# A streaming encoder step on one core: how the first conditioning rows are loaded, placed and stored

## The chip, the cores and the metric

The kernel runs on one core of a Trainium2 chip. The metric is the device time of one execution in microseconds (us). TensorE is called PE here, VectorE DVE, ScalarE ACT, GpSimd POOL and SyncE SP; SP does no arithmetic and issues most of the transfers.

## The reference

A prompt of 512 frames and eight running streams of 16 frames each (640 rows of width 2048 in all) pass through two layers, stick-breaking attention and gated linear attention. Each layer first normalises its input and shifts and scales it by a conditioning vector, one for the prompt and one for each stream. What matters for the change is that first step of the first layer:

```python
shift, scale, gate = jnp.split(c @ w_ada[i] + b_ada[i], 3, axis=-1)
h = rmsnorm(x, norm_g[i]) * (1 + scale[:, None]) + shift[:, None]
q, k, v, zg = jnp.split(h @ w_in, 4, axis=-1)
```

All is float32. `c @ w_ada` multiplies nine rows by a matrix of 2048 x 4096 for shift and scale (32 MiB in float32), so that it is a matter of moving the matrix, hardly of arithmetic.

## The kernel before

The 640 rows lie turned: rows of h (2048 of them, 16 tiles of 128) on the partitions, the 640 frames along the free dimension. To keep float32 accuracy, PE multiplies in the rounded type float32r, and each operand is split into a rounded part and a remainder (`halves`, line 133: ACT makes the rounded part, DVE the remainder), so that one product takes three matmuls.

**The beginning** (lines 758 to 848) does these things one after the other or woven together.

- x is loaded in ten pieces of 512 KB into tiles s0 to s9 of the pool `sp` (line 766). Between the first and the second pair of pieces stand six small loads: the norm weights and the bias (`crow`), and the conditioning vectors (`c9`). For each of the five groups of 128 frames (line 781), ACT squares and sums the pieces in four parts, PE turns 16 blocks, and DVE and ACT copy them out of PSUM. The reciprocal root is taken on GpSimd, and PE spreads it over the partitions (`turned_wide`, line 246).
- The conditioning matrix is taken in eight **blocks** (`ada0`, line 821, which calls `ada_mod`, line 161). A block gives shift and scale for two of the 16 tiles of h and has 4 MiB. It is loaded in 4 groups; each group is followed on PE by its small products (L180: the matrix's piece streams past the nine conditioning rows). Blocks 0, 1, 6 and 7 come alone, in pieces of 256 KB with runs of 1 KB; blocks 2 and 3, and 4 and 5, come as pairs, in pieces of 512 KB with runs of 2 KB. The pieces go round in a ring of eight tiles (s10 to s15 and two tiles `ar`), for block 6 of six, for block 7 of four (lines 817 to 819). When a block's products are done, DVE copies the sums out of PSUM (L185), PE turns them (L189), DVE adds the bias and makes scale and shift (L198 to L200).
- Then `scale` (line 405) makes two tiles of h of them (`mod`, two buffers), `part_up` (line 412) stores a half of one of them to device memory (L415, issued by ACT, ahead of the splits) and splits them, and `add_up` makes sums that later products want and writes them to tiles s2j and s2j+1 for block j.
- The **product** of block j (L519, in `six`, line 488) multiplies its two tiles of h by 512 columns of `w_in`: five groups of 128 frames, called fifths below, each with six matmuls of 512 columns. Its weights (`wr`, 512 KB) are asked for two products ahead, and their tile is free when the weights before them have been split (`wl`, L135).

After the last product begin the large ones, by a scheme with seven products in place of eight (L595, in `by_sevens`, line 529). They and all that follows are not touched by the change.

**What sets the order.** PE's queue runs in the order in which the program is written (line 81). To choose it, the program keeps a clock of its own, `pe["now"]`: each operation adds what it is held to cost (`by`, line 54), and a class `Side` (line 277) runs a side task's next step when that clock has reached its due time. For the conditioning the due time of a group comes from `pace` (line 806): the clock at which the n-th piece of 512 KB is held to have landed. The other engines and SP run in the order that the compiler's scheduler chooses, except from the end of block 7's products on, where DVE, ACT and GpSimd run as written (line 834). A queue runs strictly in order, so that a group whose piece hasn't landed holds up whatever stands behind it on PE, and a load whose tile isn't free holds up the loads behind it on SP.

Of the kernel before, what the change touches and what calls it, by code (L numbers as in the profile page):

```python
# [41 lines left out]
def hybrid_step_kernel(ctx: ExitStack, tc: tile.TileContext, A: dict, O: list):  # L42
# [4 lines left out]
    dve = nc.vector  # L47


    pe = {"now": 0.0, "quad": 4800}  # L50

    mm, turn_block = nc.tensor.matmul, nc.tensor.transpose

# [11 lines left out]
    def block(x):  # L65

        pe["now"] += 0.11
        return x
# [92 lines left out]
    def ada_mod(pool, ring, i, j0, ns, tag, group, pace=None, close=None):  # L161
# [21 lines left out]
            close()  # L183
        row = pool.tile([P, 256], F32, tag="ada_r", name="ada_r")[:, :w]
        dve.tensor_copy(row, acc[:, :w])  # L185
        yield step(1.5 if pace else 4.0, tp=1)
        tp = bank("tp")
        for s in range(ns):
            turn_block(tp[:, P * s:P * s + P], block(row[:, P * s:P * s + P]), ident)  # L189
# [38 lines left out]
    def rstd_of(pool, ss, n, name):  # L228
# [4 lines left out]
        r = pool.tile([P, w], F32, tag=name + "_r", name=name + "_r")  # L233
        nc.gpsimd.tensor_tensor(r, ms, mhalf[:, :w], op=ALU.pow)
        return r

    def rstd_row(pool, ss, bc, a):

        turned_wide(wide_of(pool, rstd_of(pool, ss, D, "nrm")), bc, a)

    def wide_of(pool, r):
        wide = pool.tile([P, P], F32, tag="rstd_w", name="rstd_w", bufs=2)
# [31 lines left out]
    def step(wait=0.0, tp=0, z=0, tiled=False):  # L274
        return wait, tp, z, tiled
# [111 lines left out]
    class Quarters:  # L387
# [24 lines left out]
        def part_up(self, i, j, two):  # L412

            (a0, a1), b = [self.exact[j][0][:, c] for c in hs], self.exact[j][1]
            nc.scalar.dma_start(out=h21_d[i][:, j, :], in_=a1)  # L415
            self.lower[j], self.upper[j] = slot(j, (P, 2, HALF)), slot(8 + j, (P, 2, HALF))
            self.whole[j] = slot(16 + 2 * j), slot(17 + 2 * j)
            halves(self.lower[j][:, 0], self.lower[j][:, 1], a0)
            halves(self.upper[j][:, 0], self.upper[j][:, 1], a1)
            halves(*self.whole[j], b)  # L420
            self.middle[j] = two[:, :P], two[:, P:]
            halves(*self.middle[j], self.exact[j][0][:, 256:384])

        def most(self, i, j, xT, t, bc, two):

# [333 lines left out]
    with tc.tile_pool(name="st", bufs=1, reuse_waits="tile") as st:  # L759
        for n, t in (("sh", sh_t), ("sc", sc_t)):  # L760
            t[0] = st.tile([P, KT, NSEQ], F32, name=f"{n}0")

        raw = {}
        crow = st.tile([120, P], F32, name="crow")
        c9 = st.tile([P, NSEQ, KT], F32, name="c9")
        for a in range(TOK):
            for hf in range(2):
                raw[a, hf] = sp.tile([P, 1024], F32, tag=f"s{2 * a + hf}", name="xr")
                load(raw[a, hf], x_src(a)[:, 1024 * hf:1024 * hf + 1024])
            if a == 0:  # L770
                load(crow[0:32, :], A["norm_g"].rearrange("l (k d) -> (l k) d", d=P))
                load(crow[32:48, :], A["gla_norm_g"].rearrange("l (k d) -> (l k) d", d=P))
                load(crow[48:56, :], A["gla_b_a"].rearrange("l (k d) -> (l k) d", d=P))
                load(crow[56:120, :], A["b_ada"][:, :2 * D].rearrange("l (k d) -> l k d", d=P))
                load(c9[:, 0, :], A["c_prompt"][0].rearrange("(p kt) -> p kt", kt=KT))
                load(c9[:, 1:, :], A["c_sample"].rearrange("r (p kt) -> p r kt", kt=KT))
        dve.tensor_copy(cT[:, :, :NSEQ], c9.rearrange("p r kt -> p kt r"))

        xT = [slot(15 + kt if kt % 2 else kt // 2, dt=F32, name="xT") for kt in range(KT)]
        bc = st.tile([P, T], F32, name="rstd_bc")  # L780
        for a in range(TOK):
            ss4 = st.tile([P, 4], F32, tag="ss4", name="ss4", bufs=2)
            for q in range(4):
                xr = raw[a, q // 2][:, 512 * (q % 2):512 * (q % 2) + 512]
                junk = st.tile([P, 512], BF16, tag="junk", name="junk")
                act(junk, xr, AF.Square, accum_out=ss4[:, q:q + 1])
# [7 lines left out]
            dve.tensor_reduce(out=ss, in_=ss4, axis=mybir.AxisListType.X, op=ALU.add)  # L794
            rstd_row(st, ss, bc, a)
            if a == 2:
                tp = bank("tp")
                nc.tensor.transpose(tp[:, :120], crow, ident[:120, :120])
                dve.tensor_copy(cols, tp[:, :120])


        pe["now"] = 30.0
        come = {"n": 0}
        ready = {}

        def pace(n):
            come["n"] += n
            return max(0.0, 18.0 + 1.4 * come["n"] - pe["now"])

        def ring(tags):  # L810
            n = 0
            while True:
                tag = tags[n % len(tags)]
                yield ad_ring() if tag is None else sp.tile([P, 1024], F32, tag=tag, name="ar")
                n += 1

        early = ring(["s10", "s11", "s12", "s13", "s14", "s15", None, None])
        late = ring(["s12", "s13", "s14", "s15", None, None])
        last = ring(["s14", "s15", None, None])

        def ada0():
            for i, (k0, n, r) in enumerate(((0, 1, early), (1, 1, early), (2, 2, early), (4, 2, early), (6, 1, late),
                                            (7, 1, last))):
                yield from ada_mod(ad, lambda: next(r), 0, k0, n, ("z", "tp")[i % 2], 2 * n, pace, in_written_order if k0 == 7 else None)
                js = range(k0, k0 + n)
                for j in js:
                    h1.scale(0, j, xT, bc, st)
                    h1.part_up(0, j, st.tile([P, 256], F32R, tag="middle", name="middle", bufs=2))
                    ready[j] = pe["now"] + 6.5 + 3.0 * (j - k0)
                    side.after(2.0 + 2.5 * (j - k0), lambda j=j: h1.add_up(j, st, (f"s{2 * j}", f"s{2 * j + 1}")))  # L830

        ends = ExitStack()

        def in_written_order():

            ends.enter_context(tc.manual_schedule(engines={mybir.EngineType.DVE, mybir.EngineType.Activation,
                                                           mybir.EngineType.Pool}))

        side.every = 0.5
        side.add(ada0())  # L840
        acc = [bank("mm") for _ in range(5)]
        drive(six(h1, w_in0, 2 * D, acc, lambda j: side.until(lambda: ready.get(j, 1e9) <= pe["now"]),
                  lambda: pace(1)))

        given = [ask_quarter(r, w_in0, D, i, j) for r, i, j in (
            (wp.tile([P, 1024], F32, tag="wr", name="wr", bufs=WR), 0, 0), (ad_ring(), 0, 1), (ad_ring(), 1, 1))]
        side.finish()
        pe["quad"] = 2400


    def rest_of_ada():
# [1258 lines left out]
```

## Time and profile before

| | |
|---|---|
| median of 3 runs | 2485.13 us (2484.14 to 2486.26) |
| the profiled execution | 2485.69 us, of which 2484.0 are its span |
| PE busy in the span | 2417.1 us (97%) |
| mean granted clock of PE | 0.991 |
| moved | 502 MB, 202 GB/s on average |
| large products (L595) begin | 152.25 us into the span |

The page divides the span into 40 slices of 62 us. The change touches the first two and a half of them:

```profile
PE   6899999999999999999999999999999999999998
PEclk8899999999999999999999999999999999999999
DMA  9966666666763348877774664444434578986634
```

Each digit is a tenth: PE is busy for 60 to 90% of the first slices and granted 0.8 of its clock, while the transfers are at 0.9 and more; later PE is full and the transfers have room. All times in the text are us from the start of the span. A row of the queue in order of time gives start, length, engine, line, operation, output<-inputs, shape, number, and in brackets the idle time before it with what ended it. A row of the waits gives who waited for whom, us in total, times, and the longest.

### The profile page before, as it was taken

How to read it: one execution, taken by the hardware profiler on the slowest of the kernel's cores; microseconds unless marked ns; L12 is line 12 of the kernel's file. 1: busy time of each engine (PE TensorE's matmuls, PEld its weight loads, DVE VectorE, ACT ScalarE, POOL GpSimd, SP SyncE). 2: the span in 40 equal slices, each digit the busy share in tenths (PEclk: the TensorE clock that was granted, in tenths of full speed). 3: DMA queues.
4: the chain of work that ended last, by engine and by line, in shares of the span. 5: the costliest groups of instructions: out<-in, count | busy, mean ns of one | idle time of the engine just before them, and what ended most of it. 6: DMA issues, size and time to landing. Idle time of an engine off the chain costs nothing.

```text
span 2484.0 us, 44037 instructions
## 1 busy us (share of the span) xinstructions
PE 2417.1 (97%) x17561; PEld 2144.7 (86%) x17561; DVE 1580.8 (64%) x2566; ACT 994.4 (40%) x1731; POOL 152.7 (6%) x397
## 2 busy tenths in 40 slices
PE   6899999999999999999999999999999999999998
PEld 4589999999999999888887767999999989977776
DVE  5575556555556665666776578766676566675556
ACT  4342222222223334555544345333333555565223
POOL 0010000000000000000000010000000132332000
PEclk8899999999999999999999999999999999999999
DMA  9966666666763348877774664444434578986634
GB/s 345 337 204 220 220 206 209 234 207 211 225 216 119 115 131 273 261 243 236 254 231 144 190 240 125 135 120 127 136 110 114 173 252 263 296 272 207 221 115 148
DMA packets 469903, 502.08 MB, mean 202 GB/s; under 512 B 26106, under 2 KB 370562, under 8 KB 469570
## 3 DMA queue, kind: packets, MB, share of 16 engines
q1 hardware_dynamic: 440338, 440.80, 55.9%
q0 software_dynamic: 14048, 45.36, 5.3%
q10 hardware_dynamic: 15312, 13.11, 1.6%
q8 instruction: 138, 2.26, 0.4%
q14 instruction: 67, 0.55, 0.1%
HBM read 410.05 MB, written 89.13 MB: 201 GB/s over the span
## 4 chain that ended last, share of the span: by engine, by line
PE 83%; DVE 3%; DMA 3%; ACT 2%; issue 2%; SPq 0%; POOL 0%; ACTq 0%; POOLq 0%; DVEq 0%
PE ps_mm L595 42%; PE ps_mm L700 10%; PE ps_mm L654 9%; PE ps_mm L369 3%; PE ps_tp L1093 2%; PE ps_tp L1572 2%; PE ps_tp L1145 1%; PE ps_tp L1049 1%; PE ps_z L1025 1%; PE ps_z L180 1%; PE ps_mm L2081 1%; PE ps_z L1107 1%; PE ps_z L222 1%; PE ps_tp L681 1%; PE ps_mm L519 1%
## 5 line engine op out<-in xcount | busy, mean ns | idle before, releaser
L595 PE MATMUL ps_mm<-sums,wh 128*128 128x320 f32 x2752 | 613.6, 311 | 1.5 <-ACT wh L134 1.5
L595 PEld LDWEIGHTS ps_mm<-sums,wh 128*128 128x128 f32 x2752 | 457.8, 188 | 10.4 <-issue 7.0
L595 PE MATMUL ps_mm<-h,wh 128*128 128x320 f32 x2064 | 461.3, 311 | 0.2 <-DVE u L601 0.2
L595 PE MATMUL ps_mm<-sums,wl 128*128 128x320 f32 x1376 | 425.3, 309 | 0.7 <-DVE wl L135 0.7
L135 DVE TENSOR_TENSOR wl<-wr,wh 128x1024 fp32r<-128x1024 f32 x193 | 236.2, 1225 | 229.4 <-ACT wh L134 228.9
L595 PEld LDWEIGHTS ps_mm<-h,wh 128*128 128x128 f32 x2064 | 343.0, 188 | 15.1 <-issue 11.3
L134 ACT CAST wh<-wb 128x1024 fp32r<-128x1024 f32 x170 | 178.4, 1049 | 433.7 <-PE ps_mm L595 369.7
L134 ACT CAST wh<-wr 128x1024 fp32r<-128x1024 f32 x193 | 202.6, 1050 | 345.2 <-PE ps_mm L595 186.1
L595 PE MATMUL ps_mm<-h,wl 128*128 128x320 f32 x1032 | 318.9, 309 | 0.0
L654 PE MATMUL ps_mm<-h,wh 128*128 128x320 f32 x1152 | 263.5, 316 | 3.4 <-ACT wh L134 1.7
L595 PEld LDWEIGHTS ps_mm<-sums,wl 128*128 128x128 f32 x1376 | 258.3, 188 | 1.0 <-DVE wl L135 1.0
L135 DVE TENSOR_TENSOR wl<-wb,wh 128x1024 fp32r<-128x1024 f32 x170 | 207.8, 1222 | 53.2 <-ACT wh L134 53.0
L654 PEld LDWEIGHTS ps_mm<-h,wh 128*128 128x128 f32 x1152 | 192.0, 188 | 17.8 <-issue 8.9
L700 PE MATMUL ps_mm<-wh,ogh 128*128 128x512 f32 x450 | 197.9, 440 | 7.5 <-ACT y L708 4.1
L595 PEld LDWEIGHTS ps_mm<-h,wl 128*128 128x128 f32 x1032 | 193.7, 188 | 0.0
L700 PE MATMUL ps_mm<-wh,ogl 128*128 128x512 f32 x450 | 178.4, 396 | 0.3 <-DVE ogl L135 0.3
L700 PE MATMUL ps_mm<-wl,ogh 128*128 128x512 f32 x450 | 178.0, 396 | 0.0
L654 PE MATMUL ps_mm<-h,wl 128*128 128x320 f32 x576 | 177.9, 309 | 0.0
L700 PEld LDWEIGHTS ps_mm<-wh,ogh 128*128 128x128 f32 x450 | 85.7, 191 | 35.5 <-issue 15.3
L654 PEld LDWEIGHTS ps_mm<-h,wl 128*128 128x128 f32 x576 | 108.2, 188 | 0.0
L700 PEld LDWEIGHTS ps_mm<-wh,ogl 128*128 128x128 f32 x450 | 85.1, 189 | 20.5 <-DVE ogl L135 0.7
L519 PE MATMUL ps_mm<-wh,h 128*128 128x512 f32 x252 | 92.2, 426 | 7.1 <-ACT h L134 3.9
(369 smaller groups left out, 3722.3 us busy)
## 6 DMA issues: line engine op xcount, KB each, us to landing
ar<-in_w_ada_dram SPq DMA_DIRECT2D x160, 512.0 KB
wb<-in_sb_w_in_dram SPq DMA_DIRECT2D x82, 512.0 KB
kc<-in_cache_sb_k_dram SPq DMA_DIRECT2D x64, 512.0 KB
vc<-in_cache_sb_v_dram SPq DMA_DIRECT2D x64, 512.0 KB
wr<-in_gla_w_in_dram SPq DMA_DIRECT2D x51, 512.0 KB
wb<-in_gla_w_in_dram SPq DMA_DIRECT2D x45, 512.0 KB
wr<-in_sb_w_in_dram SPq DMA_DIRECT2D x44, 512.0 KB
ar<-in_w_ada_dram SPq DMA_DIRECT2D x64, 256.0 KB
```

Of the source, the lines that this page charges most:

```text
L134: nc.scalar.copy(hi, x)
L135: (e or dve).tensor_tensor(lo, x, hi.bitcast(F32), op=ALU.subtract)
L180: mm(acc[32 * q:32 * q + 32, :w], cT[:, kt + m, :], by(cT[:, kt + m, :], rs[m // each][:, m % each, q, :]), start=kt + m == 0, stop=kt + m ...
L222: mm(acc[32 * j:32 * j + 32, :256], cT[:, kt + m, :], by(cT[:, kt + m, :], r[:, 256 * j:256 * j + 256]), start=kt + m == 0, stop=kt + m == ...
L369: mm(acc[a], l[:, c], by(l[:, c], r[:, k2, :]), start=kt == k0 and first, stop=kt == k0 + nk - 1 and last)
L519: mm(acc[a], l, by(l, r[:, e, :]), start=j == 0 and e == 0 and begun, stop=j == 7 and e == 1 and last)
L595: mm(acc, l[:, k, :], by(l[:, k, :], r), start=start and k == 0 and first, stop=k == 7 and last, skip_group_check=True)
L654: mm(acc[nt], l[:, k, :], by(l[:, k, :], r), start=k0 == 8 and k == 0 and first, stop=k0 == 0 and k == 7 and last)
L681: turn_block(tp[:, c:c + P], block(out[hh][:, t0:t0 + P]), ident)
L700: mm(acc, l, by(l, r[:, e, :]), start=i == 0 and e == 0 and first, stop=i == 1 and e == 1 and last)
L1093: turn_block(tp[:, P * c:P * c + P], block(kc[:, c, P * hh:P * hh + P]), ident)
L1572: mm(out, l[a], by(l[a], r[b]), start=start and n == 0, stop=stop and n == 2, skip_group_check=True)
```

## The change

- **x and the first conditioning rows in turns.** The first two groups of frames are asked for, then the conditioning vectors, then the first group of block 0, and from there a group of frames and a group of block 0 in turns. The small products of block 0 stand between the turns of x on PE. The norm weights and the bias are loaded behind the last of x.
- **Single blocks into all idle places.** All eight blocks come alone, in pieces of 256 KB and groups of two tiles. `place(j)` goes round through s10 to s15, the two tiles `ar`, and s2 to s9, and drops tiles below s2j, which the sums of block j are going to need.
- **h's rows stored from GpSimd**, behind the splits in the program.
- The pacing: a group's small products are held to cost about twice as much (`quad` 2400 in place of 4800), the n-th piece lands at 17 + 1.45 n in place of 18 + 1.4 n, the turn of a block's sums is due after 0.6 in place of 1.5, and a block's h is held to be ready 7.8 after it (6.0 for the last).
- Smaller things: squares are taken over 1024 columns at a time, with the unused h slot 8 for their output; the reciprocal root of one group of frames is spread by PE behind the turns of the next. DVE, ACT and GpSimd run in the scheduler's order as before, up to the end of block 7's products.

```diff
-    pe = {"now": 0.0, "quad": 4800}
+    pe = {"now": 0.0, "quad": 2400}
...
-        yield step(1.5 if pace else 4.0, tp=1)
+        yield step(0.6 if pace else 4.0, tp=1)
...
-            nc.scalar.dma_start(out=h21_d[i][:, j, :], in_=a1)
...
+            (move if i == 0 else nc.scalar.dma_start)(out=h21_d[i][:, j, :], in_=a1)
...
+        def pace(n):
+            come["n"] += n
+            return max(0.0, 17.0 + 1.45 * come["n"] - pe["now"])
+
+        places = [10, 11, 12, 13, 14, 15, 16, 16, 2, 3, 4, 5, 6, 7, 8, 9]
+
+        def place(j):
+            while places[0] < 2 * j:
+                places.pop(0)
+            places.append(places.pop(0))
+            return ad_ring() if places[-1] == 16 else sp.tile([P, 1024], F32, tag=f"s{places[-1]}", name="ar")
...
+        def ada0():
+            for j in range(8):
+                yield from ada_mod(ad, lambda: place(j), 0, j, 1, ("z", "tp")[j % 2], 2, pace,
+                                   in_written_order if j == 7 else None)
+                h1.scale(0, j, xT, bc, st)
+                h1.part_up(0, j, st.tile([P, 256], F32R, tag="middle", name="middle", bufs=2))
+                ready[j] = pe["now"] + (6.0 if j == 7 else 7.8)
+                side.after(2.0, lambda j=j: h1.add_up(j, st, (f"s{2 * j}", f"s{2 * j + 1}")))
+
+        ask_x(0)
+        ask_x(1)
+        load(c9[:, 0, :], A["c_prompt"][0].rearrange("(p kt) -> p kt", kt=KT))
+        load(c9[:, 1:, :], A["c_sample"].rearrange("r (p kt) -> p r kt", kt=KT))
+        rows = ada0()
+        next(rows)
...
+            wide[a] = wide_of(st, rstd_of(st, ss, D, "nrm"))
+            if a:
+                turned_wide(wide[a - 1], bc, a - 1)
+            if a == 0:
+                dve.tensor_copy(cT[:, :, :NSEQ], c9.rearrange("p r kt -> p kt r"))
+            if 1 <= a < 4:
+                ask_x(a + 1)
+                if a == 3:
+                    load(crow[0:32, :], A["norm_g"].rearrange("l (k d) -> (l k) d", d=P))
...
+                next(rows)
         pe["now"] = 30.0
...
-            for i, (k0, n, r) in enumerate(((0, 1, early), (1, 1, early), (2, 2, early), (4, 2, early), (6, 1, late),
-                                            (7, 1, last))):
...
+        next(rows)
+        tp = bank("tp")
+        nc.tensor.transpose(tp[:, :120], crow, ident[:120, :120])
+        dve.tensor_copy(cols, tp[:, :120])
+        turned_wide(wide[-1], bc, TOK - 1)
+        def more_rows():
+            yield step(0.6, tp=1)
+            yield from rows
...
-        side.add(ada0())
+        side.add(more_rows())
```

More of the change, by code (lines that the diff above doesn't have):

```diff
@@ L235, in rstd_of @@
         return r
-    def rstd_row(pool, ss, bc, a):
-        turned_wide(wide_of(pool, rstd_of(pool, ss, D, "nrm")), bc, a)
     def wide_of(pool, r):
@@ L765, in hybrid_step_kernel, with ask_x @@
         c9 = st.tile([P, NSEQ, KT], F32, name="c9")
-        for a in range(TOK):
+        def ask_x(a):
             for hf in range(2):
@@ L769, in hybrid_step_kernel @@
                 load(raw[a, hf], x_src(a)[:, 1024 * hf:1024 * hf + 1024])
[L770 to L776, printed above, removed]
@@ L777, in hybrid_step_kernel @@
-        dve.tensor_copy(cT[:, :, :NSEQ], c9.rearrange("p r kt -> p kt r"))
+        come = {"n": 0}
+        ready = {}
+        def pace(n):
[7 more added lines that the diff above has]
+            return ad_ring() if places[-1] == 16 else sp.tile([P, 1024], F32, tag=f"s{places[-1]}", name="ar")
@@ new lines, in hybrid_step_kernel, with in_written_order @@
+        ends = ExitStack()
+        def in_written_order():
+            ends.enter_context(tc.manual_schedule(engines={mybir.EngineType.DVE, mybir.EngineType.Activation,
+                                                           mybir.EngineType.Pool}))
+        def ada0():
[6 more added lines that the diff above has]
+                side.after(2.0, lambda j=j: h1.add_up(j, st, (f"s{2 * j}", f"s{2 * j + 1}")))
@@ L779, in hybrid_step_kernel @@
+        ask_x(0)
[4 more added lines that the diff above has]
+        next(rows)
         xT = [slot(15 + kt if kt % 2 else kt // 2, dt=F32, name="xT") for kt in range(KT)]
         bc = st.tile([P, T], F32, name="rstd_bc")
+        wide = [None] * TOK
         for a in range(TOK):
-            ss4 = st.tile([P, 4], F32, tag="ss4", name="ss4", bufs=2)
+            ss4 = st.tile([P, 2], F32, tag="ss4", name="ss4", bufs=2)
@@ L783, in hybrid_step_kernel @@
             for q in range(4):
+                if q % 2 == 0:
+                    junk = slot(8, (P, 1024), BF16, "junk")
+                    act(junk, raw[a, q // 2], AF.Square, accum_out=ss4[:, q // 2:q // 2 + 1])
                 xr = raw[a, q // 2][:, 512 * (q % 2):512 * (q % 2) + 512]
-                junk = st.tile([P, 512], BF16, tag="junk", name="junk")
-                act(junk, xr, AF.Square, accum_out=ss4[:, q:q + 1])
                 tp = bank("mm")
@@ L793, in hybrid_step_kernel @@
             ss = st.tile([P, 1], F32, tag="ss", name="ss", bufs=2)
[L794 to L799, printed above, removed]
-        pe["now"] = 30.0
[L803 to L821, printed above, removed]
-            for i, (k0, n, r) in enumerate(((0, 1, early), (1, 1, early), (2, 2, early), (4, 2, early), (6, 1, late),
-                                            (7, 1, last))):
[L824 to L837, printed above, removed]
+            dve.tensor_tensor(ss, ss4[:, 0:1], ss4[:, 1:2], op=ALU.add)
+            wide[a] = wide_of(st, rstd_of(st, ss, D, "nrm"))
[3 more added lines that the diff above has]
+                dve.tensor_copy(cT[:, :, :NSEQ], c9.rearrange("p r kt -> p kt r"))
@@ new lines, in hybrid_step_kernel @@
+            if 1 <= a < 4:
+                ask_x(a + 1)
+                if a == 3:
+                    load(crow[0:32, :], A["norm_g"].rearrange("l (k d) -> (l k) d", d=P))
+                    load(crow[32:48, :], A["gla_norm_g"].rearrange("l (k d) -> (l k) d", d=P))
+                    load(crow[48:56, :], A["gla_b_a"].rearrange("l (k d) -> (l k) d", d=P))
+                    load(crow[56:120, :], A["b_ada"][:, :2 * D].rearrange("l (k d) -> l k d", d=P))
+                next(rows)
+        pe["now"] = 30.0
@@ L847, in hybrid_step_kernel @@
         side.finish()
-        pe["quad"] = 2400
     def rest_of_ada():
```

## The prediction

> **What bounds the kernel now.** I read the table by stretches first, then the transfers of the first 152 us, then the PE queue in order of time, then who made SP and ACT wait. In the stretches the columns are the length, busy us (and instructions) of PE, PEld, DVE, ACT and POOL, the granted clock, the DMA share and GB/s.
>
> ```profile
> 0.00:152.00 152.00, 124.18 (x1106) 83.55 (x1107) 91.49 (x257) 63.31 (x140) 5.13 (x15) 0.90 0.90 312
> 152.00:2484.00 2332.00, 2292.96 (x16456) 2061.16 (x16454) 1489.34 (x2310) 931.11 (x1591) 147.55 (x383) 1.00 0.61 195
> ```
>
> After 152 us PE is busy 98% of the time at full clock with the transfers at 0.61: that part is bound by PE, the change leaves it alone, and whatever the beginning saves should come through whole. Before 152 us the transfers run at a share of 0.90 and 312 GB/s. How much is moved there:
>
> ```profile
> ar<-in_w_ada_dram SPq DMA_DIRECT2D x64, 256.0 KB
> ar<-in_w_ada_dram SPq DMA_DIRECT2D x32, 512.0 KB
> wr<-in_sb_w_in_dram SPq DMA_DIRECT2D x9, 512.0 KB
> xr<-in_x_prompt_dram SPq DMA_DIRECT2D x8, 512.0 KB
> h<-mod ACTq DMA_DIRECT2D x8, 160.0 KB
> xr<-in_x_sample_dram SPq DMA_DIRECT2D x2, 512.0 KB
> ```
>
> Up to the last conditioning piece that is 16 + 16 MB of `ar`, 8 x 512 KB of `wr` (the ninth belongs to what follows), 10 x 512 KB of `xr`: 41 MiB = 43.0 MB, with seven `h` stores (1.15 MB) and some 0.25 MB of small rows 44.4 MB. The speeds:
>
> ```profile
> 0.00:10.00 10.00, 3.89 (x17) 3.52 (x18) 3.29 (x16) 4.64 (x12) 1.74 (x9) 1.00 0.75 216
> 10.00:20.00 10.00, 7.42 (x33) 6.73 (x34) 4.65 (x23) 8.53 (x30) 1.10 (x2) 1.00 1.02 378
> 20.00:30.00 10.00, 6.44 (x64) 5.46 (x66) 8.40 (x40) 7.99 (x28) 1.10 (x2) 1.00 1.08 387
> 50.00:60.00 10.00, 10.00 (x93) 6.89 (x92) 5.66 (x19) 2.90 (x6) 0.00 (x0) 0.92 1.05 405
> 100.00:110.00 10.00, 7.63 (x105) 4.72 (x103) 5.12 (x14) 3.22 (x6) 0.00 (x0) 1.00 0.71 231
> 110.00:120.00 10.00, 8.22 (x54) 4.37 (x54) 6.38 (x18) 3.97 (x9) 0.00 (x0) 0.66 1.04 356
> 120.00:130.00 10.00, 10.00 (x126) 7.77 (x126) 9.70 (x24) 5.14 (x9) 0.00 (x0) 1.00 0.70 239
> ```
>
> The 20-30 stretch moves mainly 256 KB pieces of single blocks (387 GB/s), 50-60 the 512 KB pieces of double blocks (405). At such speeds 44.4 MB need some 112 us, yet the last group of pieces is used only at 135.91 (below), because the stream has holes (231, 239). Who makes them, among SP's waits of 0-160 us, in total, times, longest:
>
> ```profile
> SPq L71 <- PE ps_tp L180: 23.8, 12, 4.9
> SPq L71 <- DMA ar<-in_w_ada_dram: 19.7, 41, 2.2
> SPq L71 <- PE ps_z L180: 11.0, 11, 4.2
> SPq L71 <- DVE wl L135: 10.2, 2, 6.1
> ```
>
> Rows 1 and 3, 34.8 us, are SP waiting for a place: eight tiles go round, and a tile is free only when its block's products (L180) have run. The second row is SP waiting because the queue was full, which costs nothing. What the holes do to PE:
>
> ```profile
> 112.97 1.40 PE L180 MATMUL ps_z<-ar,cT 128*32 128x128 f32 x16 [0.25 <-DMA ar<-in_w_ada_dram]
> 114.30 0.80 PE L519 MATMUL ps_mm<-wh,h 128*128 128x512 f32 x1
> ...
> 135.91 1.08 PE L180 MATMUL ps_tp<-ar,cT 128*32 128x128 f32 x32
> 139.79 0.27 PE L189 MATMUL ps_tp<-ident,ada_r 128*128 128x128 f32 x1
> 144.56 0.50 PE L519 MATMUL ps_mm<-wh,h 128*128 128x512 f32 x1 [0.32 <-ACT h L134]
> ...
> 151.78 0.40 PE L519 MATMUL ps_mm<-wl,h 128*128 128x512 f32 x1
> 152.01 0.39 PE L519 MATMUL ps_mm<-wh,h 128*128 128x512 f32 x1
> 152.25 0.45 PE L595 MATMUL ps_mm<-h,wh 128*128 128x320 f32 x2
> ```
>
> Blocks 4 and 5 come as one; product 4 starts only at 114.30, behind pieces of block 6 that stand ahead of it on PE and land at 112.97. Four of eight products are then still to do, and PE is busy to the end of the stretch. So the beginning is **late transfers first, and PE catching up second**. At 135.91 the last group of block 7 runs, and 16.3 us later the large products (L595) begin. That time, 152.25, is what the change can move.
>
> **The change, part by part.**
>
> *Places.* Block 1 may go to eight of the tiles that held x, and with the six others and the ring of two there are 16 places instead of 8 for blocks 0 to 2, 12 for blocks 3 and 4, 8 for block 5, 6 and 4 for blocks 6 and 7 (as before for those two). With 16 places SP runs two blocks ahead, so the waits for L180 should go, except at the end. The wait for `wl` (weights two products ahead) stays, but comes when SP has over a block in flight.
>
> *Single blocks.* Blocks 2 to 5 come as 256 KB pieces: 64 more issues minus 32. An issue costs SP:
>
> ```profile
> L71 SPq DMA_DIRECT2D ar<-in_w_ada_dram x96: 367/410/1637, 11.3 to 130.2; - x96
> ```
>
> (min/median/max ns.) 128 x 0.41 = 52 us of SP, under half of the stretch; not a bound. The speed falls from 405 towards 387; with `h` stores beside I take 385 for all: 44.4 / 0.385 = 115.3 us. The ends: 405 (109.6 us) and 356, the 110-120 row, where single blocks ran at a share of 1.04 (124.7 us).
> The Trainium skill, "DMA: Bandwidth & Descriptors", section Specifications, gives some 358 GB/s as what the memory grants one core. By that figure the stream would take 124.0 us, an estimate from that page; the 387 and 405 rows here lie above it, so the measurement decides.
>
> *Order of the start.* The first 20 us moved 5.94 MB, which at 385 takes 15.4: 4.6 us are lost at the start. SP issues six small loads between the first and second x pair; after the change two, behind the second pair. I take 3.5 us lost (bounds 2.5 and 4.6). Squares on 1024 columns instead of 512, the first reduce as an add, the mean's row turned one tile later: all beside transfers, nothing.
>
> *h rows from GpSimd.*
>
> ```profile
> ACT h L134 <- DMA ar<-in_w_ada_dram: 14.1, 3, 8.1
> 152.05 0.54 POOL L78 DMA_DIRECT2D out_dram<-v  x1
> ...
> 46.67 1.32 PE L180 MATMUL ps_tp<-ar,cT 128*32 128x128 f32 x16 [1.35 <-DMA ar<-in_w_ada_dram]
> 47.93 0.80 PE L519 MATMUL ps_mm<-wh,h 128*128 128x512 f32 x1
> ```
>
> ACT stood 14.1 us in three places ahead of the split of h (L134). I read that as its own store (L415) not getting into a queue that SP keeps full; that is an inference, since the row names only a transfer. The stores leave ACT. By itself this buys little: product 0 starts at 47.93, right behind a group that waited for its transfer until 46.67. GpSimd has nothing else between 30 and 150 us, so eight issues of 0.54 us block nobody; a late store would hold only the `mod` tile, of which there are two, one full block later. I take nothing, with 0 to 3 us of gain as ends.
>
> *The planner.* The order on PE is written by a clock of the kernel's own. A group of 32 small products now costs 32 x (128/2400 + 0.01) = 2.03 us on it, a fifth of a product (6 matmuls) 6 x (512/2400 + 0.0133) = 1.36. The last group is due at 17 + 1.45 x 72 = 121.4. Carried through, this puts groups 2 and 3 of block 7 between products 5 and 6, the last group behind the second fifth of product 6, and its turn (L189), now due after 0.6, behind the third fifth. Before, two fifths stand between last group and turn. One fifth less is 6 x 0.23 = 1.4 us (matmuls at 151.78 and 152.01 start 0.23 us apart). Product 5 no longer waits for block 4 as its twin, and product 6 starts behind group 3 of block 7.
>
> *The sum.* Last piece landed: 3.5 + 115.3 = 118.8. Groups 3 and 4 of block 7 need tiles that groups 1 and 2 free, so each issue waits for a run on PE: 1.5 us, an estimate (ends 0 and 5, the longest of the waits for L180 above being 4.9). Last group at 120.3. From there 16.3 - 1.4 = 14.9 to the large products: **135.2 instead of 152.25, 17 us less**. PE has time for it: a block costs 30 x 0.23 + 2 x 1.08 = 9.1 us at full clock against 12.3 of transfers (4.72 MB / 0.385). DVE and ACT have 91.5 and 63.3 us of work, under 70% of 135. The profiled execution took 2485.69 us, 1.69 around its span of 2484.0, so it would take 2468.6; the median of the runs shown lies 0.56 lower: **2468 us**.
>
> **The rivals.**
>
> ```profile
> 83.69 1.22 PE L519 MATMUL ps_mm<-wh,h 128*128 128x512 f32 x2 [1.19 <-DVE h L135]
> 84.70 0.63 PE L519 MATMUL ps_mm<-wl,h 128*128 128x512 f32 x1
> 85.13 1.05 PE L519 MATMUL ps_mm<-wh,h 128*128 128x512 f32 x2
> ...
> 90.20 0.39 PE L519 MATMUL ps_mm<-wl,h 128*128 128x512 f32 x1
> ...
> 42.61 2.71 PE L180 MATMUL ps_tp<-ar,cT 128*32 128x128 f32 x32 [1.28 <-DMA ar<-in_w_ada_dram]
> ...
> 30.00:152.00 122.00, 66.69 (x239) 47.02 (x240) 0.87 0.88 309
> ```
>
> (The last row is the stretch for L519 alone: busy PE and PEld, clock, DMA share, GB/s.)
>
> 1. *The clock falls ahead of product 7.* Behind the last group only three fifths of product 6 are left (4 us) while h of block 7 takes some 5 us from its turn (139.79 to 144.56). A slow matmul takes 0.43 us (84.70 to 85.13), so product 7 would take 30 x 0.20 = 6 us more: start at 141, 2474 us. For it: slow stretches follow each long wait. Against: the gap is short. 20%.
>
> 2. *The pieces are slow.* At 356 GB/s the last piece comes 9.4 us later: 2477.5 us. For it: that row had a share of 1.04, so its engines were not idle. Against: 387 in 20-30. 12%.
>
> 3. *The places don't help.* SP still halts, now for `wl` or because the scheduler puts loads in another order, and the holes remain: 2483 to 2487 us, no change. Against: two waits for `wl` against 23 for places. 8%.
>
> 4. *Slower: PE at half clock all along.* Fed in drops, PE could stay slow: per block 30 x 0.43 + 64 x 0.085 (the row at 42.61) = 18.3 us, more than the 12.3 of its transfers. Product 0 can start at some 38 us (12.6 MB at 0.385, plus 3.5 and 2); eight products then end at 38 + 7 x 18.3 + 12.9 = 179: 27 us later than now, 2512 us. It decides when PE is slow for over 62% of the stretch, since 38 + 7 x (9.1 + 9.2f) + 6.9 + 6.0f = 152.25 at f = 0.62; all of the gain is gone there. Against: clock 0.87 in the row above, thus slow for a quarter, and each slow stretch ends within some 6 us of steady work (83.69 to 90.20, where a matmul's 0.63 us have become 0.39). 7%.
> The Trainium skill, "TensorE: Matmul & The Clock Gate", section HAM oscillation, says just this of thin work between transfers: each tile starts slow again. The trace agrees for the waits at 42 and 84 us, not for the whole stretch.
>
> **How the numbers follow.** The forecast has 53%, its own range 2463 to 2473: start lost 2.5 to 4.6, speed 385 to 405, ends as above. Reaching to rivals 1 and 2 gives 2460 to 2481. A change under 0.2% (5 us) can't be told from none. Faster than 2480.2: the forecast, rival 1 and most of 2: 0.80. Within: the rest of 2, and rival 3: 0.12. Slower: rival 4: 0.08.
>
> **What would show it.** Right: large products begin near 135 us; no hole under 330 GB/s between 20 and 100 us; SP's waits for L180 under 15 us, the remainder in the last 20; no wait of ACT for `ar` ahead of L134; 128 issues of 256 KB. Wrong: a DMA share under 0.9 in the middle (the places don't bind), a full share with under 370 GB/s (rival 2), clock under 0.7 over the stretch (rival 4), or a beginning that is shorter with an end that is not: then the rest was not bound by PE alone.

## The result, and the profile after

| | before | after |
|---|---|---|
| median, same chip | 2485.21 us (2483.68 to 2490.75, 6 runs) | 2473.85 us (2472.03 to 2477.33, 6 runs) |
| the profiled execution (span) | 2485.69 (2484.0) | 2472.03 (2470.1) |
| large products begin (L595, now L591) | 152.25 | 142.47 |
| the rest of the profiled time | 2333.4 | 2329.6 |

The ratio is 0.9949 [0.9939, 0.9959], 11.4 us less: faster, as forecast, but 6 us short of 2468, and with the large products at 142.5 instead of 135.2. The rest, the time behind their beginning, isn't steady: in the profiles of this study it goes from 2329.6 to 2338.0, and before's lies in the middle. So the beginning of the large products is the finer measure of an edit, and I use it beside the times. It isn't exact either: a second profile of the very same kernel has it at 140.03.

From line 241 on, the lines named here have numbers four lower in the changed kernel: product L515, large products L591, ACT's sums L463. First the table by stretches after, in the columns of the prediction:

```profile
0.00:20.00 20.00, 12.57 (x122) 10.38 (x123) 9.14 (x46) 11.63 (x28) 2.85 (x11) 1.00 0.94 322
20.00:40.00 20.00, 13.07 (x166) 7.18 (x164) 14.12 (x54) 11.31 (x27) 1.82 (x3) 0.86 1.01 358
40.00:60.00 20.00, 16.34 (x193) 11.02 (x193) 7.86 (x22) 4.97 (x9) 0.55 (x1) 0.80 1.03 355
56.00:94.00 38.00, 37.38 (x511) 28.14 (x507) 31.57 (x81) 18.94 (x34) 2.17 (x4) 1.00 1.06 372
60.00:80.00 20.00, 19.38 (x247) 14.34 (x246) 16.06 (x42) 7.73 (x14) 0.54 (x1) 1.00 1.07 376
80.00:100.00 20.00, 19.11 (x244) 13.67 (x242) 16.48 (x39) 9.76 (x18) 1.08 (x2) 1.00 1.08 382
100.00:110.00 10.00, 9.49 (x150) 6.55 (x149) 6.75 (x22) 4.50 (x8) 0.54 (x1) 1.00 1.00 333
...
130.00:140.00 10.00, 9.09 (x38) 6.37 (x37) 8.39 (x22) 5.17 (x9) 0.55 (x1) 1.00 0.59 175
```

The deep holes of before (231, 239 GB/s) are gone from the middle; what is left are dents (358, 355, 333). From 56 to 94 PE is busy for 37.38 of 38 us at full clock: it is behind the stream there, not fed by it. Next, who made SP wait in the first 160 us:

```profile
SPq L71 <- DMA ar<-in_w_ada_dram: 30.5, 87, 1.8
...
SPq L71 <- PE ps_tp L180: 5.4, 3, 3.1
...
SPq L71 <- PE ps_z L180: 3.0, 6, 1.1
```

The waits for a place (L180) fell from 34.8 to 8.4 us, and SP now waits chiefly because the queue is full. Last, the end of the beginning, on PE in order of time:

```profile
122.28 1.91 PE L180 MATMUL ps_tp<-ar,cT 128*32 128x128 f32 x56
...
124.84 0.43 PE L180 MATMUL ps_tp<-ar,cT 128*32 128x128 f32 x8 [0.66 <-DMA ar<-in_w_ada_dram]
...
128.17 1.24 PE L180 MATMUL ps_tp<-ar,cT 128*32 128x128 f32 x32
...
130.83 0.27 PE L189 MATMUL ps_tp<-ident,ada_r 128*128 128x128 f32 x1
...
142.47 0.45 PE L591 MATMUL ps_mm<-h,wh 128*128 128x320 f32 x2
```

From the last group (128.17) to the large products it takes 14.3 us, before 16.3, forecast 14.9. So the whole shortfall lies ahead of the last group, which was forecast for 120.3.

### The profile page after: what moved, and what is told of

Same layout as the page of the kernel before. It is cut to its first block, busy times and chain, and to the rows that moved or that the text cites. A ratio compares the mean times of both kernels' runs of the same rounds, so it can differ in the third digit from the quotient of the medians.

```text
span 2470.1 us, 44598 instructions
## 1 busy us (share of the span) xinstructions
PE 2408.5 (98%) x17817; PEld 2141.9 (87%) x17817; DVE 1581.7 (64%) x2580; ACT 993.3 (40%) x1711; POOL 156.6 (6%) x405
## 4 chain that ended last, share of the span: by engine, by line
PE 85%; DVE 4%; ACT 3%; DMA 2%; issue 1%; POOL 0%; SPq 0%; ACTq 0%; POOLq 0%; DVEq 0%
PE ps_mm L591 43%; PE ps_mm L696 11%; PE ps_mm L650 10%; PE ps_mm L365 3%; PE ps_tp L1100 2%; PE ps_tp L1579 2%; PE ps_tp L1152 1%; PE ps_tp L1056 1%; PE ps_z L1032 1%; PE ps_z L180 1%; PE ps_mm L2088 1%; PE ps_z L1114 1%; PE ps_z L222 1%; PE ps_tp L677 1%; PE ps_mm L515 1%
## 5 line engine op out<-in xcount | busy, mean ns | idle before, releaser
L591 PE MATMUL ps_mm<-sums,wh 128*128 128x320 f32 x2752 | 613.6, 311 | 1.5 <-ACT wh L134 1.5
L591 PEld LDWEIGHTS ps_mm<-sums,wh 128*128 128x128 f32 x2752 | 458.0, 188 | 10.4 <-issue 7.4
L591 PE MATMUL ps_mm<-h,wh 128*128 128x320 f32 x2064 | 461.4, 311 | 0.8 <-DVE u L597 0.8
L591 PE MATMUL ps_mm<-sums,wl 128*128 128x320 f32 x1376 | 425.2, 309 | 0.7 <-DVE wl L135 0.7
L591 PEld LDWEIGHTS ps_mm<-h,wh 128*128 128x128 f32 x2064 | 343.2, 188 | 15.7 <-issue 11.0
L134 ACT CAST wh<-wb 128x1024 fp32r<-128x1024 f32 x170 | 178.4, 1049 | 431.8 <-PE ps_mm L591 368.2
L134 ACT CAST wh<-wr 128x1024 fp32r<-128x1024 f32 x193 | 202.5, 1050 | 324.8 <-PE ps_mm L591 186.8
L591 PE MATMUL ps_mm<-h,wl 128*128 128x320 f32 x1032 | 318.9, 309 | 0.0
L591 PEld LDWEIGHTS ps_mm<-sums,wl 128*128 128x128 f32 x1376 | 258.3, 188 | 1.0 <-DVE wl L135 1.0
L591 PEld LDWEIGHTS ps_mm<-h,wl 128*128 128x128 f32 x1032 | 193.8, 188 | 0.0
L515 PE MATMUL ps_mm<-wh,h 128*128 128x512 f32 x252 | 90.7, 415 | 5.6 <-ACT h L134 4.0
```

The costliest lines, as they stand in the source:

```text
L134: nc.scalar.copy(hi, x)
L515: mm(acc[a], l, by(l, r[:, e, :]), start=j == 0 and e == 0 and begun, stop=j == 7 and e == 1 and last)
L591: mm(acc, l[:, k, :], by(l[:, k, :], r), start=start and k == 0 and first, stop=k == 7 and last, skip_group_check=True)
```

## The experiments

Each edit is made on the kernel after, where nothing else is said. "Begin" is the first large product in its profile.

| run | edit | begin | median us (runs) | ratio to before |
|---|---|---|---|---|
| after | | 142.47 | 2473.85 (6) | 0.9949 [0.9939, 0.9959] |
| after_again | none | 140.03 | 2474.82 (5) | 0.9958 [0.9945, 0.997] |
| e1_eight_places | eight places, not 16 | 139.22 | 2476.71 (4) | 0.9955 [0.994, 0.997] |
| e2_x_first | x and small rows all first | 142.03 | 2476.48 (4) | 0.9951 [0.9936, 0.9966] |
| e3_h_from_act | h stored from ACT as before | 152.37 | 2488.37 (10) | 0.9998 [0.9987, 1.001] |
| e9_act_behind | h stored from ACT, behind the splits | 147.38 | 2481.37 (1) | one run |
| e7_store_alone | before, with the store from GpSimd | 149.15 | 2485.64 (10) | 0.9992 [0.9983, 1.0001] |
| e10_store_and_single | e7, and all blocks single | 155.97 | 2487.99 (10) | 1.0007 [0.9997, 1.0018] |
| e11_old_clock | the planner's clock of before | 148.72 | 2481.73 (1) | one run |
| e4_small_apart | small rows loaded from GpSimd | 140.95 | 2474.64 (4) | 0.9942 [0.9927, 0.9957] |
| e6_both | e4, and other places for blocks 6 and 7 | 142.87 | 2474.04 (5) | 0.9949 [0.9936, 0.9963] |
| e8_eight_small | e4 with eight places | 138.01 | 2471.61 (5) | 0.9942 [0.9928, 0.9955] |
| e8_again | the same | 138.32 | 2471.18 (6) | 0.9945 [0.993, 0.9959] |

The theory at first was the prediction's: the places carry the gain. The rivals: the order of x carries it, or the store that left ACT.

**Is it the places?**

```diff
-        places = [10, 11, 12, 13, 14, 15, 16, 16, 2, 3, 4, 5, 6, 7, 8, 9]
+        places = [10, 11, 12, 13, 14, 15, 16, 16]
```

> The changed kernel with only the eight old tiles for the pieces (s10 to s15 and the two ar), everything else of the change kept. Theory (places): the gain is made by the 16 places; without them SP waits for L180 again for some 30 us instead of 8.4, the stream has holes, and the large products begin at 148 to 152 us instead of 142.5; 2479 to 2485 us. Rival (order and single blocks): what helps is that blocks come alone and that PE's order is another; then the large products stay within 2 us of 142.5.

It isn't. With the eight places of before the large products begin at 139.22, if anything earlier, the interval of the time overlaps that of after, and SP's waits for L180 are no longer than after's:

```profile
SPq L71 <- PE ps_tp L180: 6.0, 9, 2.5
...
SPq L71 <- PE ps_z L180: 1.6, 4, 0.9
```

7.6 us with eight places, 8.4 with 16. So eight places are enough once the rest is changed, and the 34.8 us of before weren't a lack of places alone.

**Is it the turns of x?**

```diff
-        ask_x(0)
-        ask_x(1)
-        load(c9[:, 0, :], A["c_prompt"][0].rearrange("(p kt) -> p kt", kt=KT))
-        load(c9[:, 1:, :], A["c_sample"].rearrange("r (p kt) -> p r kt", kt=KT))
+        for a in range(TOK):
+            ask_x(a)
+            if a == 0:
+                load(crow[0:32, :], A["norm_g"].rearrange("l (k d) -> (l k) d", d=P))
...
+                load(c9[:, 1:, :], A["c_sample"].rearrange("r (p kt) -> p r kt", kt=KT))
...
-            if 1 <= a < 4:
-                ask_x(a + 1)
...
-                next(rows)
+        for _ in range(3):
+            next(rows)
```

> The changed kernel with all of x, the norm rows and the conditioning vectors asked for first, in the order of before, and the small products of block 0 behind the turns of x; places, single blocks and stores as changed. Theory (the stream is the bound): x has to come anyway, so the order of the start moves the large products by the 1 to 2 us that SP's small loads cost between the first x pieces: 143 to 145 us. Rival (the start is what was won): product 0 begins 5 us or more later than its 39.7 and the large products with it, 147 us or later.

Not that either: 142.03, with product 0 at 40.68, and the same time within the intervals.

**Is it the store of h?** In e3 the store goes back to ACT, ahead of the splits:

```diff
             (a0, a1), b = [self.exact[j][0][:, c] for c in hs], self.exact[j][1]
+            nc.scalar.dma_start(out=h21_d[i][:, j, :], in_=a1)
...
-            (move if i == 0 else nc.scalar.dma_start)(out=h21_d[i][:, j, :], in_=a1)
```

> The changed kernel with h's rows stored by ACT again, ahead of the splits. Theory: the store waits behind SP's full queue, ACT stands again ahead of the split of h (14 us in three places before, more now that the queue is never empty: 20 us or more), the products start later and PE, which has less slack than the stream, loses 3 to 8 us: the large products begin at 145 to 150 us. Rival (my step of the prediction, which took 0 to 3 us for it): they stay within 142 to 145 us because the stream is late anyway.

All of the gain is gone, more than the run's theory had it: 152.37, ratio 0.9998 [0.9987, 1.001]. Here the chain can be read off. ACT's queue in e3, in order of time:

```profile
36.81 0.29 ACT L134 CAST middle<-mod 128x128 fp32r<-128x128 f32 x1
55.64 0.35 ACTq L411 DMA_DIRECT2D h<-mod  x1
56.03 1.08 ACT L134 CAST h<-mod 128x320 fp32r<-128x320 f32 x2 [18.93 <-DMA ar<-in_w_ada_dram]
```

SP's queue in the same stretch:

```profile
36.36 14.66 SPq L71 DMA_DIRECT2D ar<-in_w_ada_dram  x22
51.34 2.37 SPq L71 DMA_DIRECT2D ada_bg<-in_b_ada_dram  x4
54.36 1.06 SPq L71 DMA_DIRECT2D wr<-in_sb_w_in_dram  x2
59.90 1.90 SPq L71 DMA_DIRECT2D ar<-in_w_ada_dram  x4
```

And PE, once product 0 had begun at 40.33:

```profile
57.17 0.80 PE L515 MATMUL ps_mm<-wh,h 128*128 128x512 f32 x1 [15.19 <-ACT h L134]
```

ACT is done at 37.1 and its store gets out at 55.64, as soon as SP has stopped (54.36 + 1.06 = 55.42). While SP keeps issuing into a full queue, ACT's store stands, the split of h stands behind it, and PE stands 15.19 us in the middle of product 0. Before it was the same thing, smaller. ACT's store there, behind its longest wait (8.1 us):

```profile
46.71 0.34 ACTq L415 DMA_DIRECT2D h<-mod  x1
```

and SP's queue, between two issues of which it got out:

```profile
45.97 0.37 SPq L71 DMA_DIRECT2D ar<-in_w_ada_dram  x1
...
47.36 1.72 SPq L71 DMA_DIRECT2D ar<-in_w_ada_dram  x3
```

Here SP had not stopped: from 46.34 to 47.36 it waited at the full queue itself, and the store got in ahead of its next issue. That gap may be what the store made and not what let it in. Nine issues of SP had passed the store by then, in e3 26. So the rows show that ACT's store can stand as long as SP keeps a full queue supplied, and that it can also get in earlier; what decides it isn't settled, and no run changed the length of SP's run alone. From GpSimd the store costs one issue; the last of the eight in the changed kernel:

```profile
135.25 0.55 POOL L78 DMA_DIRECT2D h<-mod  x1 [15.41 <-ACT h L134]
```

GpSimd waited only until DVE or ACT was done with h, never for a transfer. The Trainium skill, "DMA: Bandwidth & Descriptors", section Issuing engines are not separate DMA queues, says that issuing from several engines saves no more than the sequencer's issue time, which is usually small. In e3 it wasn't small: with SP's queue full, the one issue held ACT for 18.93 us.

In e9 it goes to ACT too, but stays behind the splits:

```diff
-            (move if i == 0 else nc.scalar.dma_start)(out=h21_d[i][:, j, :], in_=a1)
+            nc.scalar.dma_start(out=h21_d[i][:, j, :], in_=a1)
```

> The changed kernel with h's rows stored by ACT, but behind the splits as the changed kernel has it. Theory (ACT can't issue while SP keeps the queue full, wherever the store stands): ACT stands for 10 us or more at the store of block 0, now ahead of the rounded sums and of block 1's second step instead of the splits; product 0 starts on time (39 to 41 us), product 1 late (58 us or later instead of 52.2), and the large products begin at 147 us or later. Rival (only the place ahead of the splits hurts): they begin within 2 us of 142.5.

With the store behind the splits (one run) ACT stands about as long, but now ahead of the sums; among the waits of e9:

```profile
ACT sums L463 <- DMA ar<-in_w_ada_dram: 17.8, 1, 17.8
```

The large products begin at 147.38, half of the loss. Product 0 starts on time (39.73). Product 1 isn't late to start, as was expected, but begins at 51.94 and stands in the middle until after 59. So in these two runs the halt comes from the engine that issues, and what it costs from what stands behind it.

**Is the store enough?** e7 makes the same edit in the kernel before, with nothing else of the change.

```diff
-            nc.scalar.dma_start(out=h21_d[i][:, j, :], in_=a1)
...
+            (move if i == 0 else nc.scalar.dma_start)(out=h21_d[i][:, j, :], in_=a1)
```

> The kernel before with one edit alone: h's rows of the first layer are stored by GpSimd behind the splits. Theory (the store is one of two parts that need each other): ACT's waits of 14.1 us go, but eight old places, double blocks and the old order on PE still leave SP waiting for L180 and product 0 behind the group that lands at 46.67; the large products begin at 147 to 150 us, 2480 to 2483 us. Rival A (the store is all of the gain): they begin at 141 to 144, 2473 to 2477 us. Rival B (the store is worth nothing by itself, as the prediction had it): within 1 us of 152.25.

No: 149.15, 3.1 us earlier as expected, but a time (2485.64, expected 2480 to 2483) whose interval includes 1. SP still waits for places:

```profile
SPq L71 <- PE ps_tp L180: 23.2, 9, 6.2
...
SPq L71 <- PE ps_z L180: 11.2, 12, 4.2
```

**Are single blocks what is missing?** e10 adds them to e7, with eight places and the old clock and start.

```diff
-            for i, (k0, n, r) in enumerate(((0, 1, early), (1, 1, early), (2, 2, early), (4, 2, early), (6, 1, late),
-                                            (7, 1, last))):
+            for i, (k0, n, r) in enumerate(((0, 1, early), (1, 1, early), (2, 1, early), (3, 1, early),
+                                            (4, 1, early), (5, 1, early), (6, 1, late), (7, 1, last))):
```

> The kernel before with two edits: h's rows of the first layer stored by GpSimd behind the splits, and blocks 2 to 5 taken alone, in 256 KB pieces, instead of in pairs. Places (eight), order of the start, the clock of the planner as before. Theory (these two are what the change consists of): with no pair to wait for, products 2 to 5 follow their blocks, SP's waits for L180 fall from 34 us to under 15, and the large products begin at 141 to 145 us; 2473 to 2478 us. Rival (the planner's new clock is the second part): they begin at 147 us or later, as with the store alone (149.2).

Not by themselves: 155.97, 6.8 us later than e7, and SP's waits for L180 stay at 28.4 us. PE in e10:

```profile
47.58 1.34 PE L180 MATMUL ps_tp<-ar,cT 128*32 128x128 f32 x16 [1.35 <-DMA ar<-in_w_ada_dram]
48.85 0.80 PE L519 MATMUL ps_mm<-wh,h 128*128 128x512 f32 x1
...
92.13 0.73 PE L519 MATMUL ps_mm<-wh,h 128*128 128x512 f32 x2 [1.50 <-DVE h L135]
...
105.67 0.73 PE L519 MATMUL ps_mm<-wh,h 128*128 128x512 f32 x2 [1.49 <-DVE h L135]
```

The old order puts product 0 behind groups of block 1 that land at 47.58, and products 2 to 5 so close to their h that PE waits 1.5 us inside each; the blocks follow at 13.5 us (92.13 to 105.67), slower than the 12.3 us in which the prediction has the stream bring one. e11 keeps all of the change but the clock:

```diff
-    pe = {"now": 0.0, "quad": 2400}
+    pe = {"now": 0.0, "quad": 4800}
...
-        yield step(0.6 if pace else 4.0, tp=1)
+        yield step(1.5 if pace else 4.0, tp=1)
...
-            return max(0.0, 17.0 + 1.45 * come["n"] - pe["now"])
+            return max(0.0, 18.0 + 1.4 * come["n"] - pe["now"])
...
-                ready[j] = pe["now"] + (6.0 if j == 7 else 7.8)
+                ready[j] = pe["now"] + 6.5
...
+        pe["quad"] = 2400
```

> The changed kernel with the planner's old costs: quad 4800, landing at 18 + 1.4 n, turn after 1.5, ready after 6.5. Theory (single blocks and the store carry it, the clock only shifts who stands first): large products within 2 us of 142.5. Rival (the clock is the second part): 146 us or later.

148.72 (one run), as the rival had it: the new clock is worth 6.2 us (8.7 against after_again). The tail shows most of it. PE's turns of blocks 6 and 7 in e11, and its large products:

```profile
117.48 0.27 PE L189 MATMUL ps_tp<-ident,ada_r 128*128 128x128 f32 x1
...
135.49 0.28 PE L189 MATMUL ps_tp<-ident,ada_r 128*128 128x128 f32 x1
...
148.72 0.45 PE L591 MATMUL ps_mm<-h,wh 128*128 128x320 f32 x2
```

The first is 1.7 us later than after's (115.74), the second 4.7 (130.83), the last 6.2. From e10 to e11, 7.3 us, lie the new start and the places. Neither the places alone (e1) nor the order of the loads (e2) matters on the changed kernel; what remains, by elimination, is that block 0's groups are written ahead of the clock's start, so that product 0 begins at 39.9 (e11) and not at 48.85. No run had that part alone, nor the new clock with pairs of blocks.

**What made the dents?** Where the transfers are slow after (26 to 30 and 54 to 58), SP has just issued four small loads each time, the norm weights and the bias (`crow`) from 19.27 on and the bias of the gate from 51.60 on:

```profile
19.27 0.34 SPq L71 DMA_DIRECT2D crow<-in_norm_g_dram  x1
...
51.60 2.53 SPq L71 DMA_DIRECT2D ada_bg<-in_b_ada_dram  x4
```

e4 sends these eight from GpSimd.

```diff
-                load(bias[32 * j:32 * j + 32, :], A["b_ada"][i, n0:n0 + 256].partition_broadcast(32))
+                move(bias[32 * j:32 * j + 32, :], A["b_ada"][i, n0:n0 + 256].partition_broadcast(32))
...
-                    load(crow[0:32, :], A["norm_g"].rearrange("l (k d) -> (l k) d", d=P))
+                    move(crow[0:32, :], A["norm_g"].rearrange("l (k d) -> (l k) d", d=P))
```

> The changed kernel with the four loads of the norm rows and the bias rows of the gate issued by GpSimd instead of SP. Theory (small loads take places in SP's queue): the holes at 26 to 30 us (265 to 280 GB/s) and 54 to 58 us (233 to 317) go, the stretch 20 to 60 us moves at 375 GB/s or more, and the large products begin 2 to 3 us earlier, near 140. Rival: the holes come from tiles that aren't free or from the speed of the pieces themselves; they stay, and so does 142.5.

The same two stretches after:

```profile
26.00:30.00 4.00, 3.01 (x41) 2.14 (x39) 2.92 (x15) 2.92 (x9) 0.55 (x1) 1.00 0.82 272
54.00:58.00 4.00, 4.00 (x54) 2.75 (x56) 2.68 (x10) 1.52 (x3) 0.00 (x0) 0.90 0.87 275
```

and in e4:

```profile
26.00:30.00 4.00, 3.22 (x42) 2.52 (x42) 2.30 (x13) 2.65 (x7) 0.55 (x1) 1.00 1.07 393
54.00:58.00 4.00, 4.00 (x41) 2.77 (x41) 1.69 (x8) 0.40 (x1) 0.00 (x0) 0.68 1.06 389
```

So these dents were the small loads in SP's queue. But the 2 to 3 us expected of it don't show: the beginning, 140.95, stays within what after itself shows (142.47, 140.03), and the time within its interval.

**And the end?** e6 adds to e4 other places for blocks 6 and 7, so that block 7 has more of them; e8 takes e4 with eight places.

```diff
+        own = {6: [12, 13, 10, 11, 14, 15, 16, 16], 7: [14, 15, 12, 13, 16, 16, 14, 15]}
+
         def place(j):
+            if j in own:
+                n = own[j].pop(0)
+                return ad_ring() if n == 16 else sp.tile([P, 1024], F32, tag=f"s{n}", name="ar")
```

> The changed kernel with the small loads issued by GpSimd and with other tiles for blocks 6 and 7, so that the last group of block 7 reuses tiles of its first group (free at the first small products of block 7) instead of those of its second (free behind product 5). Theory (the stream is the bound to the end): the last group runs 2 to 3 us earlier than 128.2 for each of the two edits, the large products begin at 138 to 139.5 us, 2470 us or a little more. Rival (PE's written order is the bound there): 141 us as with the small loads alone.

```diff
-        places = [10, 11, 12, 13, 14, 15, 16, 16, 2, 3, 4, 5, 6, 7, 8, 9]
+        places = [10, 11, 12, 13, 14, 15, 16, 16]
...
-                    load(crow[0:32, :], A["norm_g"].rearrange("l (k d) -> (l k) d", d=P))
+                    move(crow[0:32, :], A["norm_g"].rearrange("l (k d) -> (l k) d", d=P))
```

> The changed kernel with the eight old places and the small loads issued by GpSimd. Theory (more than eight places buy nothing once the store is off ACT): the same as with sixteen places within the spread, large products at 138 to 142 us. Rival (the places matter and the run with eight was lucky): 145 us or later.

e6 bought nothing (142.87 in place of 138 to 139.5). e8 has the fastest stream of all from 20 to 100 us and the earliest beginning. Its middle, and its last group of pieces on PE:

```profile
20.00:100.00 80.00, 73.11 (x952) 50.13 (x945) 56.73 (x170) 35.43 (x71) 4.43 (x8) 0.94 1.08 386
```

```profile
123.62 1.33 PE L180 MATMUL ps_tp<-ar,cT 128*32 128x128 f32 x32
```

After had its last group at 128.17, and in the same stretch moved 368 GB/s:

```profile
20.00:100.00 80.00, 67.90 (x845) 46.21 (x842) 54.51 (x154) 33.77 (x65) 3.99 (x7) 0.91 1.05 368
```
To see whether the difference holds, both ran again, unchanged.

> The changed kernel once more, to see how far its beginning moves between executions and to stand beside the version with eight places on one chip. Theory (the beginning is steady): large products within 1 us of 142.5. Rival (it moves by several us, and the 3 us between sixteen and eight places are chance): 139 to 141 or 144 and later.

> The version with eight places and the small loads issued by GpSimd once more, beside the changed kernel. Theory (more places cost the stream some speed): large products within 1 us of 138.0 and 3 to 5 us ahead of the changed kernel, 0.1 to 0.2% in time. Rival (chance): within 2 us of it.

e8 begins at 138.01 and 138.32, after at 142.47 and 140.03. So after's beginning moves by 2.4 us, as the first run's rival had it, and the two new runs are 1.7 us apart, within what the second run's rival allows to chance. The medians point the same way (2471.6 and 2471.2 against 2473.9 and 2474.8), but the intervals of the ratios overlap, so neither an earlier beginning nor a gain in time is shown. e8 has the lowest medians of all. What goes with the beginning is how much has been moved by 110 us (the mean GB/s of that stretch times its length): 39.2 MB in after, 39.4 in e2, 39.9 in after_again, 40.4 in e1 and e4, 40.9 in both runs of e8. Only e6 (40.3), where the end was changed too, falls out of that row.

Why eight places do no worse than 16 isn't settled. With 16, the scheduler puts the loads in another order, and in the profile after PE waits for the last group of block 1:

```profile
48.20 1.34 PE L180 MATMUL ps_tp<-ar,cT 128*32 128x128 f32 x16 [2.20 <-DMA ar<-in_w_ada_dram]
```

No run had that order alone.

Taken together: the store away from ACT (without it 152.4) and the new clock (without it 148.7, one run) are both needed, and so, as far as e10 against e11 tells, is the early product 0. The store alone gives 3.1 us. The extra places and the order of x carry none that shows. Whether pairs of blocks would have done under the new clock stays open.

## Why the prediction was right or wrong

**Way and size.** The time fell as forecast. 2473.85 lies within the wide range (2460 to 2481) and 0.85 us above the forecast's own (2463 to 2473); of the 17 us of the beginning 9.8 came, 12.2 in the second profile. But it did not fall for the reason given first: the places carry nothing that shows, and the store, which was set at nothing, is the part without which the gain is gone. So the right way is in part luck.

**The bound: right.** The rest came through whole. Behind the large products' beginning nothing changed beyond what differs from profile to profile, and the gain in time (11.4) is about that of the beginning (9.8 and 12.2 in the two profiles).

**The start: right.** 322 GB/s for 20 us are 6.44 MB, which at 385 take 16.7: 3.3 us lost, forecast 3.5.

**The speed: right, but not for all of the time.** Where nothing disturbed it the stream ran at 376 to 382 GB/s (386 in e8), forecast 385. The Trainium skill's 358 for one core ("DMA: Bandwidth & Descriptors", Specifications) bound nothing here. The dents (272 and 275 GB/s) were not foreseen. By 110 us the rows above add up to 39.2 MB, where (110 - 3.5) x 0.385 gives 41.0: 1.8 MB, or 4.7 us late.

**The last four pieces: too low.** I took 1.5 us for the waits of block 7's last groups. Its groups 2 and 3 stand on PE behind a product until 122.28, the tiles for group 4 come free only with group 2, and SP's last eight issues took from 116.74 to 125.54. That leaves 7.9 - 4.7 = 3.2 us more than forecast. e8 bears this split out: it had moved 40.9 MB by 110 us (372 GB/s), as much as forecast, and its last group still ran at 123.62, 3.3 us late.

**The end from the last group: right**, 14.3 against 14.9. The turn came earlier, as worked out.

**The places: wrong, though their sign came true.** "With 16 places ... the waits for L180 should go": they went, from 34.8 to 8.4 us, but with eight places too (7.6). What the row showed was true, that SP waited until L180 had run. I read it as too few tiles; it was products that ran late, since L180 stood on PE behind others: with all 16 places the waits came back when the store went to ACT (e3, 13.8 + 4.9 = 18.7 us) or the old clock was kept (e11, 11.3 + 3.1 = 14.4). Rival 3 had this half right (the places don't help) and its time wrong, since other parts helped. (By `place`, block 4 has ten places and not 12; nothing hangs on it.)

**The planner: too small.** I counted 1.4 us for its turn and let the rest follow. e11 puts it at 6.2 (one run), and without it and the early product 0 single blocks end 6.8 us later than pairs (e10 against e7).

**h's rows from GpSimd: wrong.** "I take nothing, with 0 to 3 us of gain as ends." On the kernel before that holds: e7 gave 3.1 us at the beginning and no time that can be told from none. In the change it is the part without which all is lost (e3). I had read ACT's 14.1 us rightly as its own store standing before a full queue, and took it as a constant. But a halt isn't a constant of the store: with the rest of the change SP issues from 28.18 to 55.42 almost without a break, and the longest halt grew from 8.1 to 18.9 us.

**PE's slack: mis-sized, and this is why the store mattered.** I gave a block 30 x 0.23 + 2 x 1.08 = 9.1 us of PE, against 12.3 of transfers. The matmuls' term was right. But a block has four groups of 32 records, not two. From PE's queue after, two groups together, and the next product:

```profile
57.67 1.95 PE L180 MATMUL ps_z<-ar,cT 128*32 128x128 f32 x64
59.56 0.50 PE L515 MATMUL ps_mm<-wh,h 128*128 128x512 f32 x1
```

Four groups are 4 x 0.95 = 3.8 us, the product 6.9, and with the turn and the changes between them it comes to 11.55: so far apart are two turns in e3, where PE had all its pieces and only caught up.

```profile
101.83 0.28 PE L189 MATMUL ps_tp<-ident,ada_r 128*128 128x128 f32 x1
...
113.38 0.27 PE L189 MATMUL ps_tp<-ident,ada_r 128*128 128x128 f32 x1
```

PE makes up 12.3 - 11.55 = 0.75 us a block, not 3.2. By my figure a halt of 15 us would have been made up within five blocks, and the store could indeed be left out of the sum. By the measured one seven blocks make up 5.2 of the 15.19 us, and 10.0 are left; e3 began 9.9 later than after (152.37 against 142.47). That the two agree so closely is luck, since against the second profile e3 is 12.3 later; 3.2 us a block would have left nothing either way. Rival 4 has the same slip, 64 records of a block for 128.

**The rivals.** Rival 1 gave the numbers that came (141 and 2474), but not by its mechanism: from 60 to 140 us the granted clock is 1.00 in every stretch. Nor did rival 2 come, though its sign, a full share with under 370 GB/s, is met by the letter (1.05 and 368 from 20 to 100 us): where no small loads were in the way the pieces ran at 376 and 382. Rival 4 did not come: the clock was 0.86 and 0.80 between 20 and 60 us and full from there on.

**What was to show it.** Waits for L180 under 15 us, none of ACT for `ar` ahead of L134, 128 issues of 256 KB: all so. The beginning near 135 and no hole under 330: neither (142.5; 272 and 275). The waits for L180 did fall, but not by the places, and only e1 showed that.

## What to carry to other kernels

Where a small store can be held up beside a stream, try it on an engine on which no compute waits behind it. A halt that is short in the trace of before can grow under the change that is being priced, so it isn't a constant. A wait for a buffer says that its reader ran late, which may be the order on the reader's engine and not the number of buffers: try fewer buffers before crediting more. And before a cost is called hidden, count the slack of the engine that has to make it up, from two like marks in the trace, not from parts.

## What the runs showed of the hardware

- A store issued from ACT can be held up while SP issues into a full queue: 8.12 us (before), 18.93 (e3), 17.8 (e9). The same eight stores from GpSimd waited for no transfer (after).
- Four small loads in SP's queue (`crow` 4 to 32 KB each) cost the stream far more than their bytes: 272 and 275 GB/s for 4 us behind them, against 393 and 389 with these loads issued from GpSimd (e4).
- Two executions of one kernel differ by 2.4 us in the first 142 (142.47 and 140.03), so a change of 2 us in a beginning has to be read from more than one profile. Over the profiles of all kernels the rest of the time differs by up to 8.4 us (2329.6 to 2338.0). The three longest are those of e3, e7 and e10; whether that is chance or the kernels isn't shown.
